# Some elementwise work of a two-layer trunk may go to GpSimd, and a 42-row mask matmul is padded to 128 rows

## The chip, the core and the metric

The program runs on one core of a Trainium2 chip. The metric is the device time of one execution in microseconds. Three executions of the kernel before took 3345.6, 3346.67 and 3353.66 us; the median, 3346.67 us, is what the prediction starts from.

## The reference

Two layers of a latent-diffusion trunk run over 1024 latent tokens and 256 context tokens of width 1024. Each layer normalises and modulates the stream, projects it once with `w_in`, gives the columns to four head groups, joins their outputs with `w_out` and adds them back, and then runs a squared-ReLU MLP of width 4096. Cut to what the change touches:

```python
u = modulate(rms_norm(h, norm1_g), mod[0], mod[1])
pa, pb, pc, pd = jnp.split(u @ w_in, IN_SPLITS, axis=-1)
ya = ssd_bidir(pa)              # Mamba-2 scan by chunks of 128, both directions
yb = attention(rope(norm(q)), rope(norm(k)), v)
a = jnp.exp(log_a)              # RG-LRU
u = jnp.sqrt(-jnp.expm1(2.0 * log_a)) * (i * xr)
h = linear_scan(a, u, h0)
yc = gelu(gate) * (h_fwd + h_bwd)
yd = rms_norm(o1 - lam * o2) * (1 - lam_init)
h = h + mod[2] * (jnp.concatenate([ya, yb, yc, yd], -1) @ w_out)
h = h + mod[5] * (jnp.square(relu(v @ w_mlp1)) @ w_mlp2)
```

The second layer does not update the context tokens.

## The kernel before

**The arithmetic.** Large matmuls are done three times: a float32 operand is split into a high half, rounded to the type fp32r (a one-pass matmul type), and a low half, which is the difference. Then high by high, high by low and low by high are accumulated in one PSUM bank. So each weight block that comes in as `wr` gets a `wh` (a copy with rounding) and a `wl` (a subtraction); this is `split_w` (line 878). Head-group outputs are split in the same way into `yh` and `yl` (`split_mix`, line 1031) or into the two parts of a tile `mo` (`attn_out`, line 1488).

**The stages of a layer.** `ORDER` (line 651) writes them down: the RG-LRU of the first half of its channels, its second half beside the projection of the differential values, the projection `dtq` (step sizes and the queries of the grouped attention), two groups of the SSD, the projections `dk` and `dq`, two rounds of attention, and the output projection in two parts. Then the MLP follows.

- `lru_tile` (line 1092) works on tiles of 128 channels by 1284 columns (latent tokens, a gap, context tokens). For each of two directions it makes gates with ScalarE, then products (`a0 * q`, `thr * a0`, `thi * thr`, in the trace tiles `a` and `th`) and then a scan on VectorE. At the end it forms the gated output `gw`.
- `ssd_group` (line 1190) handles ten chunks in layer 0 and eight in layer 1, for two groups, so 36 chunks. For each chunk a matmul spreads one row of cumulative decays over all partitions. The rows lie in the tile `acr` at partitions 0 to 9 (high halves) and 32 to 41 (low halves); the weights are a one-hot column of `pick`, broadcast. Only 42 partitions take part.
- `qk_post` (line 1297) squares, sums, rotates and transposes queries and keys. The rotation makes two products and adds them (`qkw<-qkw`). The power of -0.5 in every norm runs on GpSimd.

**The order of issue.** Every instruction is first recorded as an operation with an estimated cost in ns. `due` (line 380) gives each a latest time, counted back from TensorE's own order. `run` (line 414) then plays the engines against each other and emits the instructions of each engine in the order found; on the chip every engine's queue is fixed, and semaphores hold the dependences. An operation can have alternatives on two engines (`either`, ScalarE or VectorE). Where an operation is ready, line 512 keeps it back from an engine if another would end it sooner, costs being weighted by `PREF` (line 161):

```python
if any(max(t, free[a], o.ready[a]) + o.alts[a][1] * self.PREF[a]
       < t + o.alts[e][1] * self.PREF[e]
       for a in o.alts if a != e):
```

In the profile all instructions of this planner have one line, L606 (in the order of the changed kernel, L613), since one helper emits them. They are told apart by the names of their tiles; `banks` is PSUM.

Of the kernel before, what the change touches and what calls it, by code (L numbers as in the profile page):

```python
# [11 lines left out]
F32R = mybir.dt.float32r  # L12
AF = mybir.ActivationFunctionType
ALU = mybir.AluOpType
# [141 lines left out]
class Sched:  # L156
# [3 lines left out]
    TABLES = {AF.Sqrt: 1, AF.Exp: 0, AF.Tanh: 0, AF.Abs: 0}  # L160
    PREF = dict(ACT=1.0, DVE=1.6)

# [125 lines left out]

# [1 line left out]
    def act_cost(self, out, in_, func, **kw):  # L290
# [33 lines left out]
    def either(self, out, in_, act, dve):  # L324
        fast = in_.t.cls != "psum"
        a, d = dict(out=out, in_=in_, **act), dve
        ca = self.act_cost(**a)
        cd = self.dve_cost(d[0], fast, **d[1])
        o = self.op("ACT", [("activation", a)], min(ca, cd))
        o.alts = {"ACT": (o.calls, ca), "DVE": ([d], cd)}  # L330
        return o

# [45 lines left out]

# [1 line left out]
    def due(self):  # L380
# [267 lines left out]
class Trunk:  # L648
# [25 lines left out]

# [1 line left out]
    def setup(self):  # L676
        s, A = self.s, self.A
        self.cst = self.const(448, "cst")
        s.dma(self.cst.v, A["cst"])
        c = self.cst  # L680
        self.ident, self.mf, self.mb = c[:, 0:128], c[:, 128:256], c[:, 256:384]
        self.blk2, self.inv_ln, self.inv128 = c[:, 384:386], c[:, 386:387], c[:, 387:388]
        self.nhalf, self.tiny, self.ones32 = c[:, 388:404], c[:, 404:405], c[:, 406:438]
        self.pick = self.const(10, "pick", dt=F32R)[0:42, :]
        s.copy("DVE", self.pick, c[0:42, 438:448])
        self.cT = self.const(8 * 32, "cT")
        self.consts_a(0)
        x = s.tile("h", 512, F32, "load", "cx")
        s.copy("DVE", x[:, 0:16], self.crow)
        s.act(x[:, 16:32], x[:, 0:16], AF.Exp, scale=-1.0)  # L690
        s.ts(x[:, 16:32], x[:, 16:32], 1.0, None, ALU.add)
        s.dve("reciprocal", out=x[:, 16:32], in_=x[:, 16:32])
        s.op("POOL", [("memset", dict(ap=self.cT.v, constant=0.0))], 300)
        s.tt(self.cT.v.r("p (k c) -> p k c", c=32)[:, :, 0:2].r("p k c -> p c k"),
             x[:, 0:16].r("p (c k) -> p c k", c=2), x[:, 16:32].r("p (c k) -> p c k", c=2), ALU.mult)
# [180 lines left out]

# [1 line left out]
    def split_w(self, raw, n):  # L878
        s = self.s
        hi = s.tile("w", WW, F32R, "", "wh")  # L880
        s.copy("ANY", hi[:, 0:n], raw[:, 0:n])
        lo = s.tile("w", WW, F32R, "", "wl")
        s.tt(lo[:, 0:n], raw[:, 0:n], hi[:, 0:n].f, ALU.subtract)
        return hi, lo
# [53 lines left out]

# [1 line left out]
    def load_x(self, gi):  # L940
# [90 lines left out]
    def split_mix(self, k, x, n, stream):  # L1031
        s = self.s
        hi = s.tile("S", SW, F32R, stream, "yh")
        s.copy("ANY", hi[:, 0:n], x[:, 0:n])
        lo = s.tile("S", SW, F32R, stream, "yl")
        s.tt(lo[:, 0:n], x[:, 0:n], hi[:, 0:n].f, ALU.subtract)
        self.save_mix(k, hi, lo, n)
# [9 lines left out]

# [1 line left out]
    def conv(self, out, raw, wcols, bcol, W=CW):  # L1049
# [28 lines left out]

# [1 line left out]
    def lru_weights(self, l):  # L1080
# [11 lines left out]
    def lru_tile(self, l, ct, raw, gate, bd, wy):  # L1092
        s, L = self.s, self.L[l]
        xc = s.tile("S", SW, F32, "lru", "xc")
        self.conv(xc, raw, [L["lcw"][:, 2 * j + ct:2 * j + ct + 1] for j in range(4)], L["lcb"][:, ct:ct + 1])
        hs = []
        W = CW
        for d in range(2):
# [3 lines left out]
            for wi, bn in ((0, "hbr"), (1, "hbi")):  # L1102
                t = s.tile("S", SW, F32, "lru", "th")
                wv = bd[:, 128 * (4 * wi + 2 * d + ct):128 * (4 * wi + 2 * d + ct) + 128]
                for a, b in ((0, 512), (512, 1024), (1024, CW)):
                    pb = s.tile("psum", 512, F32, "lru", "pl")
# [3 lines left out]
            thr, thi = th  # L1110
            m4, p2 = L["m4"][:, idx:idx + 1], L["p2"][:, idx:idx + 1]
            a0 = s.tile("S", SW, F32, "lru", "a0")
# [3 lines left out]
            q = s.tile("S", SW, F32, "lru", "q")  # L1116
            s.stt(q[:, 0:W], thr[:, 0:W], 1.0, a0[:, 0:W], ALU.add, ALU.mult)
            s.affine(q[:, 0:W], q[:, 0:W], -1.0, 2.0)
            s.tt(a0[:, 0:W], a0[:, 0:W], q[:, 0:W], ALU.mult)
            s.act(thr[:, 0:W], thr[:, 0:W], AF.Sqrt, bias=self.tiny)  # L1120
            s.stt(thi[:, 0:W], thi[:, 0:W], 1.0, xc[:, 0:W], ALU.add, ALU.mult)
            s.tt(thr[:, 0:W], thr[:, 0:W], a0[:, 0:W], ALU.mult)
            s.tt(thi[:, 0:W], thi[:, 0:W], thr[:, 0:W], ALU.mult)
            s.affine(a0[:, 0:W], a0[:, 0:W], 2.0, -1.0)
# [19 lines left out]
        g, w = gate[:, 0:wy], s.tile("S", SW, F32, "lru", "gw")  # L1144
        wv = w[:, 0:wy]
        s.act(wv, g, AF.Square)
        s.affine(wv, wv, 0.044715, 1.0)
        s.tt(wv, wv, g, ALU.mult)
        s.act(wv, wv, AF.Tanh, scale=math.sqrt(2.0 / math.pi))
        s.stt(g, wv, 1.0, g, ALU.add, ALU.mult)  # L1150
        s.tt(wv, hs[0][:, 0:wy], hs[1][:, 0:wy], ALU.add)
        s.stt(wv, wv, 0.5, g, ALU.mult, ALU.mult)
        self.split_mix(4 + ct, w, wy, "lru")

# [1 line left out]
    def ssd_dt(self, l, dtraw):  # L1156
        s, L = self.s, self.L[l]
        c = self.ssdc
        dt, dta, w1, w2, w3 = (c[:, 80 * i:80 * i + 80] for i in range(5))
        nac, dec, te = w3, w2, w1  # L1160
        x = dtraw
# [15 lines left out]
        R = s.tile("S", SW, F32R, "ssdr", "acr")  # L1177
        s.op("POOL", [("memset", dict(ap=R[0:42, 0:1024].f, constant=0.0))], 1300)
        n4 = nac.r("p (t d g h) -> p g d h t", t=10, d=2, g=2)
# [10 lines left out]
    def ssd_group(self, l, g, xs, B, C, zmake):  # L1190
# [37 lines left out]
        for i, c in enumerate(order):  # L1228
# [5 lines left out]
            pb = s.tile("psum", 512, F32, "ssd", "pbc")  # L1234
            s.mms([dict(out=pb.v, lhsT=self.pick[:, c:c + 1].bc([42, 128]), rhs=self.acr[0:42, 512 * g:512 * g + 512],
                        start=True, stop=True)])
# [58 lines left out]

# [1 line left out]
    def qk_post(self, l, bank, off, H, d, gain, t, dst, rq=None):  # L1297
# [16 lines left out]
        if t < 8:  # L1314
            j = d // 4
            o = 144 * t + (0 if d == 64 else 96)
            cs = self.rope[:, o:o + d // 2]
            sn = self.rope[:, o + d // 2:o + d + d // 2]
            b4, c4, s4 = (v.r("p (h f k) -> p h f k", h=H, f=2) for v in (b, c, st[:, 0:n]))
            s.tt(c4, b4, cs.un(1).un(1).bc([128, H, 2, 2 * j]), ALU.mult)  # L1320
            s.tt(s4, b4[:, :, ::-1], sn.r("p (f k) -> p f k", f=2).un(1).bc([128, H, 2, 2 * j]), ALU.mult)
            s.tt(b, c, st[:, 0:n], ALU.add)
        y = b
# [49 lines left out]

# [1 line left out]
    def att_open(self, l, kind, idx):  # L1375
# [112 lines left out]
    def attn_out(self, st, b0, nb):  # L1488
# [28 lines left out]
        s.copy("ANY", hi, o[:, 0:n])  # L1517
        s.tt(lo, o[:, 0:n], hi.f, ALU.subtract)
        for d, v in zip(st["mix"], (hi, lo)):
# [9 lines left out]

# [1 line left out]
    def out_proj(self, l, gis, ks):  # L1531
# [242 lines left out]
```

## Time and profile before

| what | value |
|---|---|
| median of three executions | 3346.67 us |
| lowest and highest | 3345.6 and 3353.66 us |
| profiled execution, span from first to last instruction | 3352.2 us |
| TensorE busy | 3258.6 us (97%) |
| VectorE busy | 2171.1 us (65%), 3785 instructions |
| ScalarE busy | 1166.4 us (35%) |
| GpSimd busy | 147.1 us (4%), 168 instructions |
| mean granted TensorE clock | 0.990 |

A profile is of one execution, and the profiled one is a run of its own: its span is 5.5 us above the median of the runs that were timed. Busy time of TensorE is from the start of a matmul to its modelled end, and matmuls overlap, so that the step from one start to the next tells what a matmul really takes. Engines are called PE (TensorE), DVE (VectorE), ACT (ScalarE) and POOL (GpSimd) in the rows.

### The profile page before, as it was taken

What the parts mean: (1) busy time and instruction counts of PE and PEld (TensorE: products, weight loads), DVE (VectorE), ACT (ScalarE), POOL (GpSimd) and SP (SyncE); (2) the same over time, 40 slices, a digit from 0 to 9 for tenths busy, and PEclk for the clock granted to TensorE, in tenths of its full rate; (3) what the DMA queues carried; (4) which work ended last, traced back from release to release, by engine and by line L of the source; (5) the groups of instructions that cost most, each with busy time, mean ns of one, the idle gap of its engine ahead of it and who ended that gap; (6) DMA issues with size and microseconds to landing.
All of it is one profiled execution on the core that took longest, in us unless ns stands there. A gap on an engine that the chain in (4) does not pass through costs nothing. (4 is left out here: it accounts for less than half of the span.)

```text
span 3352.2 us, 45841 instructions
## 1 busy us (share of the span) xinstructions
PE 3258.6 (97%) x18456; PEld 2622.8 (78%) x18456; DVE 2171.1 (65%) x3785; ACT 1166.4 (35%) x2026; POOL 147.1 (4%) x168
## 2 busy tenths in 40 slices
PE   8999989999999999999999999999999999999999
PEld 6877786677688888887887888886677788888887
DVE  4787789894565555554556688689883655555554
ACT  5554447772311110101112554438771311111111
POOL 0010040000000000000000010030000000000000
PEclk9999999999999999999999989989999999999999
DMA  8443261416212222212110321151433111111111
GB/s 247 140 125 97 89 175 41 110 35 232 70 48 75 72 79 67 78 57 85 42 45 26 118 73 50 57 154 39 97 116 121 41 51 51 51 44 46 49 50 57
DMA packets 253868, 276.51 MB, mean 82 GB/s; under 512 B 22876, under 2 KB 212184, under 8 KB 253656
## 3 DMA queue, kind: packets, MB, share of 16 engines
q1 hardware_dynamic: 253656, 273.59, 27.0%
q8 instruction: 145, 2.38, 0.3%
q14 instruction: 67, 0.55, 0.1%
HBM read 218.75 MB, written 54.79 MB: 82 GB/s over the span
## 5 line engine op out<-in xcount | busy, mean ns | idle before, releaser
L606 DVE SCALAR_TENSOR_TENSOR hR<-banks,mod,hR 128x512 f32<-128x512 f32 x720 | 497.2, 697 | 420.4 <-PE banks L606 420.4
L606 PE MATMUL banks<-uh,wh 128*128 128x512 f32 (+1 forms) x1808 | 682.4, 377 | 5.8 <-ACT cvr L606 1.9
L606 PE MATMUL banks<-uh,wl 128*128 128x512 f32 (+1 forms) x1808 | 669.1, 370 | 1.7 <-DVE wl L606 1.7
L606 PE MATMUL banks<-ul,wh 128*128 128x512 f32 (+1 forms) x1808 | 669.0, 370 | 1.3 <-DVE ul L606 1.2
L606 ACT ACTIVATE wh<-wr 128x1024 fp32r<-128x1024 f32 (+2 forms) x193 | 189.5, 992 | 1050.7 <-PE banks L606 1009.9
L606 PE MATMUL banks<-hh,wh 128*128 128x512 f32 (+1 forms) x1280 | 476.7, 372 | 0.0
L606 PE MATMUL banks<-hl,wh 128*128 128x512 f32 (+1 forms) x1280 | 475.5, 371 | 0.0
L606 PE MATMUL banks<-hh,wl 128*128 128x512 f32 (+1 forms) x1280 | 474.8, 371 | 0.0
L606 PEld LDWEIGHTS banks<-uh,wh 128*128 128x128 f32 x1808 | 341.3, 189 | 98.8 <-issue 26.1
L606 PEld LDWEIGHTS banks<-uh,wl 128*128 128x128 f32 x1808 | 340.6, 188 | 65.4 <-DVE wl L606 3.0
L606 PEld LDWEIGHTS banks<-ul,wh 128*128 128x128 f32 x1808 | 341.1, 189 | 61.5 <-DVE ul L606 3.7
L606 DVE TENSOR_SCALAR_CACHE_REDUCE P<-banks,rq 128x1280 f32<-128x1280 f32 (+1 forms) x216 | 301.3, 1427 | 29.4 <-PE banks L606 28.1
L606 DVE TENSOR_TENSOR r<-r 128x512 f32<-128x512 f32 x160 | 102.2, 639 | 333.6 <-ACT r L606 331.4
L606 PEld LDWEIGHTS banks<-hh,wh 128*128 128x128 f32 x1280 | 240.8, 188 | 53.5 <-DVE hR L606 5.3
L606 ACT ACTIVATE P<-P,am 128x1280 f32<-128x1280 f32 (+1 forms) x216 | 273.4, 1272 | 21.1 <-DVE P L606 19.8
L606 PEld LDWEIGHTS banks<-hh,wl 128*128 128x128 f32 x1280 | 240.4, 188 | 44.7
L606 PEld LDWEIGHTS banks<-hl,wh 128*128 128x128 f32 x1280 | 240.6, 188 | 43.3
L606 PE MATMUL banks<-wh,uh 128*128 128x256 f32 (+2 forms) x784 | 250.4, 319 | 6.0 <-DVE qkw L606 4.2
L606 DVE TENSOR_TENSOR wl<-wr,wh 128x1024 fp32r<-128x1024 f32 (+2 forms) x204 | 230.4, 1137 | 27.6 <-ACT wh L606 26.1
L606 PE MATMUL banks<-ks,qt 128*128 128x512 f32 (+1 forms) x800 | 220.8, 387 | 20.2 <-DVE P L606 15.7
L606 PE MATMUL banks<-wl,uh 128*128 128x256 f32 (+2 forms) x784 | 226.3, 289 | 0.0
L606 PE MATMUL banks<-wh,ul 128*128 128x256 f32 (+2 forms) x784 | 225.5, 288 | 0.0
(241 smaller groups left out, 4341.0 us busy)
## 6 DMA issues: line engine op xcount, KB each, us to landing
wr<-in_w_mlp_dram SPq DMA_DIRECT2D x128, 512.0 KB
wm<-in_w_mod_dram SPq DMA_DIRECT2D x96, 512.0 KB
wr<-in_w_in_dram SPq DMA_DIRECT2D x40, 512.0 KB
ks<-dk SPq DMA_DIRECT2D x64, 160.0 KB
qt<-dq SPq DMA_DIRECT2D x72, 128.0 KB
wr<-in_w_out_dram SPq DMA_DIRECT2D x64, 128.0 KB
hd<-hT SPq DMA_DIRECT2D x8, 640.0 KB
ks<-gk SPq DMA_DIRECT2D x16, 320.0 KB
```

The source lines that it names most:

```text
L606: getattr(e, method)(**args)
```

## The change

An operation of two tensors may now be given to VectorE or GpSimd (`tt_any`), where the planner's line 512 takes its choice. The weights of the choice are 1.6 for VectorE and 0.7 for GpSimd, with a cost of 150 + 2.2 n on GpSimd and 69 + 1.0417 n on VectorE for n columns. The low halves in `split_w`, `split_mix` and `attn_out`, five products and sums in `lru_tile` and the sum of the rotation in `qk_post` are recorded in this way. Apart from that, the matmul of the decays takes all 128 rows, with zeros in the added ones.

```diff
-    PREF = dict(ACT=1.0, DVE=1.6)
+    PREF = dict(ACT=1.0, DVE=1.6, POOL=0.7)
+    POOL_TT = 2.2
...
+    def tt_any(self, out, in0, in1, op):
+        o = self.tt(out, in0, in1, op)
+        kw = dict(out=out, in0=in0, in1=in1, op=op)
+        o.alts = {"DVE": (o.calls, o.cost), "POOL": ([("tensor_tensor", kw)], 150 + self.POOL_TT * out.n())}
+        return o
...
-        self.pick = self.const(10, "pick", dt=F32R)[0:42, :]
-        s.copy("DVE", self.pick, c[0:42, 438:448])
+        self.pick = self.const(10, "pick", dt=F32R)
+        s.copy("DVE", self.pick.v, c[:, 438:448])
...
-        s.tt(lo[:, 0:n], raw[:, 0:n], hi[:, 0:n].f, ALU.subtract)
+        s.tt_any(lo[:, 0:n], raw[:, 0:n], hi[:, 0:n].f, ALU.subtract)
...
-            s.tt(a0[:, 0:W], a0[:, 0:W], q[:, 0:W], ALU.mult)
+            s.tt_any(a0[:, 0:W], a0[:, 0:W], q[:, 0:W], ALU.mult)
...
-            s.tt(thr[:, 0:W], thr[:, 0:W], a0[:, 0:W], ALU.mult)
-            s.tt(thi[:, 0:W], thi[:, 0:W], thr[:, 0:W], ALU.mult)
+            s.tt_any(thr[:, 0:W], thr[:, 0:W], a0[:, 0:W], ALU.mult)
+            s.tt_any(thi[:, 0:W], thi[:, 0:W], thr[:, 0:W], ALU.mult)
...
-        s.op("POOL", [("memset", dict(ap=R[0:42, 0:1024].f, constant=0.0))], 1300)
+        s.op("POOL", [("memset", dict(ap=R[:, 0:1024].f, constant=0.0))], 1300)
...
-            s.mms([dict(out=pb.v, lhsT=self.pick[:, c:c + 1].bc([42, 128]), rhs=self.acr[0:42, 512 * g:512 * g + 512],
+            s.mms([dict(out=pb.v, lhsT=self.pick[:, c:c + 1].bc([128, 128]), rhs=self.acr[:, 512 * g:512 * g + 512],
...
-            s.tt(b, c, st[:, 0:n], ALU.add)
+            s.tt_any(b, c, st[:, 0:n], ALU.add)
```

Two more products and sums of `lru_tile` (`wv`) and the low halves in `split_mix` and `attn_out` change in the same words.

What the planner makes of it shows in the engines' queues. On VectorE, in the first direction of the first LRU tile of layer 0, this stood before (`q` and `th` are inputs of the scan, which is the row with two inputs named `a` and `th`):

```order
L606 TENSOR_SCALAR a_433_1040<-a_433_1040 128x1284
L606 SCALAR_TENSOR_TENSOR q_1067<-th_1023,a_433_1040 128x1284
L606 TENSOR_SCALAR q_1067<-q_1067 128x1284
L606 TENSOR_TENSOR a_433_1040<-a_433_1040,q_1067 128x1284
L606 SCALAR_TENSOR_TENSOR th_1038<-th_1038,xc_968 128x1284
L606 TENSOR_TENSOR th_1023<-th_1023,a_433_1040 128x1284
L606 TENSOR_TENSOR th_1038<-th_1038,th_1023 128x1284
L606 COPY vv_1077<-banks 128x256
L606 SCALAR_TENSOR_TENSOR q_1067<-a_433_1040,th_1038 128x256
```

And this stands there now:

```order
L613 TENSOR_SCALAR a_433_1040<-a_433_1040 128x1284
L613 SCALAR_TENSOR_TENSOR q_1067<-th_1023,a_433_1040 128x1284
L613 TENSOR_SCALAR q_1067<-q_1067 128x1284
L613 SCALAR_TENSOR_TENSOR th_1038<-th_1038,xc_968 128x1284
L613 COPY vv_1077<-banks 128x256
L613 TENSOR_SCALAR a_433_1040<-a_433_1040 128x1284
L613 SCALAR_TENSOR_TENSOR th_1129<-th_1129,xc_968 128x1284
L613 SCALAR_TENSOR_TENSOR q_1067<-a_433_1040,th_1038 128x256
```

The three products have left VectorE's queue, and the scan stands behind work of the other direction. They are on GpSimd, between weight halves:

```order
L613 TENSOR_TENSOR wl_1021<-wr_939,wh_1017 128x1024
L613 TENSOR_TENSOR a_433_1040<-a_433_1040,q_1067 128x1284
L613 TENSOR_TENSOR th_1023<-th_1023,a_433_1040 128x1284
L613 TENSOR_TENSOR th_1038<-th_1038,th_1023 128x1284
L613 MEMSET q_1067 128x4
L613 TENSOR_TENSOR a_458_1158<-a_458_1158,q_1193 128x1284
```

In the projection `dq` of layer 0 GpSimd's queue held the powers `rq` alone, one for each tile of tokens. Now the sum of the rotation stands between them:

```order
L613 TENSOR_TENSOR rq_1531<-qkm_4410,cst_66 128x8
L613 TENSOR_TENSOR qkw_4421<-qkw_4421 128x256
L613 TENSOR_TENSOR rq_1531<-qkm_4447,cst_66 128x8
L613 TENSOR_TENSOR qkw_4462<-qkw_4462 128x256
L613 TENSOR_TENSOR rq_1531<-qkm_4492,cst_66 128x8
```

Each sum follows the power of its own tile and stands ahead of the power of the next. Over the whole program 234 operations move from VectorE to GpSimd: 169 low halves of weights (139 of 1024 columns, one of 1056, 29 of 512), 22 products of the LRU (8 `a`, 14 `th`), 3 `gw`, 4 `yl`, 13 `mo` and 23 sums of the rotation. Some copies also change sides: ScalarE's 48 casts `hh` become 3, VectorE's 112 become 157.

## Rows read from the trace of the kernel before

**Rows 1.** The page's first part: busy time and share of the span.
```profile
PE 3258.6 (97%) x18456; PEld 2622.8 (78%) x18456; DVE 2171.1 (65%) x3785; ACT 1166.4 (35%) x2026; POOL 147.1 (4%) x168
```
**Rows 2.** Busy time by stretch: length, engines (instructions), granted clock, DMA share, GB/s.
```profile
84.00:252.00 168.00, 163.63 (x1050) 136.12 (x1049) 133.74 (x195) 90.72 (x131) 17.73 (x26) 0.99 0.41 132
252.00:504.00 252.00, 240.53 (x1640) 201.28 (x1638) 199.16 (x517) 114.24 (x280) 46.20 (x43) 0.96 0.41 121
...
924.00:1764.00 840.00, 840.00 (x4387) 691.66 (x4386) 447.71 (x736) 108.36 (x147) 0.00 (x0) 1.00 0.21 65
1848.00:2016.00 168.00, 162.35 (x941) 137.63 (x941) 123.28 (x182) 89.56 (x133) 15.14 (x17) 0.95 0.30 96
2016.00:2268.00 252.00, 236.90 (x1532) 204.03 (x1530) 204.05 (x505) 111.88 (x264) 41.20 (x42) 0.95 0.31 87
...
2604.00:3276.00 672.00, 669.81 (x2892) 537.20 (x2891) 371.32 (x501) 116.85 (x148) 2.02 (x2) 1.00 0.17 47
```
**Rows 3.** Who TensorE waited for, 84 to 504 us: us, times, longest.
```profile
PE banks L606 <- DVE wk L606: 4.9, 2, 3.8
PE banks L606 <- DVE qkw L606: 3.3, 3, 1.7
```
**Rows 4.** The same view, 1850 to 2268 us.
```profile
PE banks L606 <- DVE qkw L606: 6.7, 6, 2.5
...
PE banks L606 <- DVE wk L606: 2.2, 4, 1.1
```
**Rows 5.** TensorE in order of time, around 2055 us: start, length, matmul.
```profile
2055.07 0.28 PE L606 MATMUL banks<-wl,uh 128*128 128x256 f32 x1
2055.20 0.28 PE L606 MATMUL banks<-wh,ul 128*128 128x256 f32 x1
2055.41 0.49 PE L606 MATMUL banks<-acr,pick 42*128 42x512 f32 x1
2055.82 0.38 PE L606 MATMUL banks<-wh,uh 128*128 128x256 f32 x1
2056.05 0.28 PE L606 MATMUL banks<-wl,uh 128*128 128x256 f32 x1
```
**Rows 6.** The same view, two matmuls of 512 columns on 128 rows.
```profile
2040.75 0.39 PE L606 MATMUL banks<-uh,wh 128*128 128x512 f32 x1
2040.98 0.40 PE L606 MATMUL banks<-ul,wh 128*128 128x512 f32 x1
```
**Rows 7.** Groups by line on TensorE: count | busy us, mean ns | idle before.
```profile
L606 PE MATMUL banks<-uh,wl 128*128 128x512 f32 x1408 | 556.7, 395 | 1.7 <-DVE wl L606 1.7
...
L606 PE MATMUL banks<-acr,pick 42*128 42x512 f32 x36 | 18.0, 501 | 0.7 <-DVE xs L606 0.7
```
**Rows 8.** The same view of VectorE: a weight's low half, an LRU product, the rotation's sum.
```profile
L606 DVE TENSOR_TENSOR wl<-wr,wh 128x1024 fp32r<-128x1024 f32 x168 | 203.4, 1220 | 26.8 <-ACT wh L606 26.1
...
L606 DVE TENSOR_TENSOR qkw<-qkw 128x256 f32<-128x256 f32 x48 | 20.2, 420 | 0.6
...
L606 DVE TENSOR_TENSOR th<-th,th 128x1284 f32<-128x1284 f32 x8 | 11.9, 1494 | 0.2
```
**Rows 9.** The same view of GpSimd: powers of the norms, and a memset.
```profile
L606 POOL TENSOR_TENSOR qkm<-qkm,cst 128x8 f32<-128x8 f32 x20 | 34.0, 1704 | 167.3 <-DVE qkm L606 167.3
...
L606 POOL MEMSET bd<- 128x1024 f32 x2 | 1.9, 952 | 1.0 <-PE banks L606 1.0
```
**Rows 10.** GpSimd in order of time, one power at 161.68 and one at 170.50 us.
```profile
161.68 1.01 POOL L606 TENSOR_TENSOR rq<-qkm,cst 128x4 f32<-128x4 f32 x1 [28.49 <-DVE qkm L606]
...
170.50 2.18 POOL L606 TENSOR_TENSOR rq<-qkm,cst 128x4 f32<-128x4 f32 x1 [3.38 <-DVE qkm L606]
```
**Rows 11.** VectorE in order of time at the second of them.
```profile
170.33 1.49 DVE L606 TENSOR_TENSOR a<-a,q 128x1284 f32<-128x1284 f32 x1
171.73 1.49 DVE L606 SCALAR_TENSOR_TENSOR th<-th,xc 128x1284 f32<-128x1284 f32 x1
```

More of the change, by code (lines that the diff above doesn't have):

```diff
@@ L1035, in split_mix @@
         lo = s.tile("S", SW, F32R, stream, "yl")
-        s.tt(lo[:, 0:n], x[:, 0:n], hi[:, 0:n].f, ALU.subtract)
+        s.tt_any(lo[:, 0:n], x[:, 0:n], hi[:, 0:n].f, ALU.subtract)
         self.save_mix(k, hi, lo, n)
@@ L1147, in lru_tile @@
         s.affine(wv, wv, 0.044715, 1.0)
-        s.tt(wv, wv, g, ALU.mult)
+        s.tt_any(wv, wv, g, ALU.mult)
         s.act(wv, wv, AF.Tanh, scale=math.sqrt(2.0 / math.pi))
         s.stt(g, wv, 1.0, g, ALU.add, ALU.mult)
-        s.tt(wv, hs[0][:, 0:wy], hs[1][:, 0:wy], ALU.add)
+        s.tt_any(wv, hs[0][:, 0:wy], hs[1][:, 0:wy], ALU.add)
         s.stt(wv, wv, 0.5, g, ALU.mult, ALU.mult)
@@ L1517, in attn_out @@
         s.copy("ANY", hi, o[:, 0:n])
-        s.tt(lo, o[:, 0:n], hi.f, ALU.subtract)
+        s.tt_any(lo, o[:, 0:n], hi.f, ALU.subtract)
         for d, v in zip(st["mix"], (hi, lo)):
```

## The prediction, made before the changed kernel had run

> **What bounds the kernel.** I read the page's busy shares first: TensorE is busy 97% of the span, VectorE 65%, GpSimd 4% [rows 1]. So time can go only where TensorE sits idle or runs slowly, and the view by stretch says where that is. In the two MLP stretches TensorE is busy 840.00 of 840 us and 669.81 of 672 us at clock 1.00, while VectorE is at 53 and 55% [rows 2]: work taken off VectorE there buys nothing. What is left are four stretches. In 84:252 and 1848:2016 the RG-LRU runs, VectorE is busy 133.74 and 123.28 of 168 us, and TensorE idles 4.4 and 5.7 us. In 252:504 and 2016:2268 the SSD and the projections `dk` and `dq` run; VectorE has 199.16 and 204.05 of 252 us, and TensorE idles 11.5 and 15.1 us [rows 2]. The view of waits names VectorE's `wk` and `qkw` for 4.9 + 3.3 us in the first half of these and 6.7 + 2.2 us in the second, together 17.1 us [rows 3, 4].
>
> A second loss sits in the same stretches. The clock has two levels, 1.2 and 2.4 GHz; its mean is 0.99, 0.96, 0.95 and 0.95 there [rows 2], and half of full speed is missing whenever it is low: 0.01 x 168 + 0.04 x 252 + 0.05 x 168 + 0.05 x 252 = 32.8 us of lost matmul time. In the MLP, where TensorE never idles, the clock does not fall. So the most that a relief of VectorE could return is 17.1 us of waits and some of the 32.8 us.
>
> **The padding.** Around a 42-row matmul the starts are 2055.20, 2055.41, 2055.82 and 2056.05 [rows 5]: steps of 0.21, 0.41 and 0.23 us. Elsewhere a matmul of 256 columns steps by 0.13 us (2055.07 to 2055.20) [rows 5] and one of 512 columns on 128 rows by 0.23 us [rows 6]. The three steps would be 0.13 + 0.23 + 0.13 = 0.49 instead of 0.85 us, so the odd shape costs 0.36 us, and there are 36 of them [rows 7]: 13.0 us at most. Counting only the matmul's own step (0.41 against 0.23) it is 6.5 us; nothing, if TensorE waits for `wk` behind it anyway. I take 9 us, near the middle of the two counts, since TensorE is busy 95% of 252:504. The memset of `acr` takes all 128 partitions and the same 1024 columns; it costs nothing more, being off every wait.
>
> **The price of a two-input instruction on GpSimd.** The trace has none of more than 10 columns. Its powers take 1704 ns for 8 columns [rows 9], about 0.2 us a column; at that rate a half of 1024 columns would take 200 us. That is the upper end, to which I give no weight: a power is a function to be computed, a subtraction one pass. The memset writes 1024 columns in 952 ns [rows 9], 0.93 ns a column; it reads nothing, so 0.95 us is the lower end. I take three such streams, two read and one written, as the memset is the nearest row: 2.86 us for 1024 columns, 3.58 us for 1284, 0.71 us for 256. VectorE takes 1.22, 1.49 and 0.42 us [rows 8].
>
> The Trainium skill's GPSIMD Engine Reference, section 3.1, gives 4497 ns for an add of 2048 columns, which would be an estimated 2.25 us for 1024 and 2.82 us for 1284 (no run here shows it yet).
>
> **The LRU stretches.** In 84:252, 15 instructions of 1284 columns (11 products, two `gw`, two `yl`) and 7 `wl` leave VectorE: 15 x 1.49 + 7 x 1.22 = 31 us, so it falls from 134 to 103 us. GpSimd gets 15 x 3.58 + 7 x 2.86 = 74 us. In 1848:2016, 11 products, one `gw` and 8 `wl` leave: 27 us, from 123 to 96; GpSimd gets about 65 us. If the two engines ran freely beside each other, that is a clear relief.
>
> Rows speak against that. A power on four columns takes 1.01 us at 161.68, but 2.18 us at 170.50 [rows 10], while VectorE runs a product of two SBUF tiles from 170.33 to 171.82 [rows 11]. The 1.17 us too many are the 1.32 us that this product still had to run, but for a small start-up. VectorE's next instruction, again of two SBUF tiles, ran its usual 1.49 us meanwhile. So GpSimd is held while VectorE reads two tiles. The other direction is not shown, as a power reads only a few columns; I bound it between no hold and a hold for the whole GpSimd instruction. Nearly everything in the LRU reads two SBUF tiles. With some hold, VectorE gives back what it won: saved 31 and 27 us, held for up to 74 and 65. I put the net on the end of the program at 0 in my forecast, and keep both ends, as rivals below.
>
> The Trainium skill (SBUF — State Buffer, section "Who interferes with whom") says that a VectorE instruction with two SBUF inputs and a GpSimd one that reads SBUF exclude each other for a whole instruction, whichever starts first. Rows 10 and 11 agree for the side where VectorE is first; by the full rule the third case below would be the forecast.
>
> **The other moves.** *Rotation sums:* 23 move. In `dq` GpSimd then has 1.70 + 0.71 = 2.4 us a tile, TensorE 24 matmuls of 0.13 us, 3.1 us: it fits, so 0. Behind a late sum stand the next tile's power and, on TensorE, its transposes; if the cover goes, half a microsecond for each of 23 tiles, 12 us. *Weight halves in the MLP:* 110 of 1024 columns. TensorE waited 1.7 us in total for `wl` in the commonest form [rows 7], since halves are made a block ahead, and a block of the first MLP matmul lasts 24 steps of 0.23 us, 5.5 us. An added 1.6 us is covered; without cover it would be 110 x 1.6 = 180 us. GpSimd has nothing else to do there. *`mo`:* 13 halves in attention, read by a store, at nothing. *Casts:* 45 `hh` more on VectorE; at 53 to 55% it has room. No queue of DMA issues is lengthened; the loads of weights wait a little longer for a `wr` tile read by a later half, with a DMA share of 0.17 to 0.21 there [rows 2].
>
> The sum is -9 us. The profiled execution's span of 3352.2 us stands 5.5 us above the median, so I take the difference off the median: 3346.67 - 9 = 3338 us. Its own range is 3326 to 3350.
>
> **Rivals.** *The relief is real* (no hold worth speaking of). VectorE loses a fifth of its load in the LRU; waits and the low clock halve: 8.5 + 16.4 us, with the padding -34 us, 3313 us. For it: VectorE was never slowed by a power. Against: those read next to nothing.
>
> *GpSimd becomes the brake.* The two exclude each other. In 84:252 the remaining 103 us and GpSimd's 74 us make 177, 9 more than the 168 us there are; in 1848:2016, 96 + 65 = 161 fits. Besides, the scans stand behind the products in VectorE's fixed queue: 22 products, each 2.1 us longer, 46 us of which half reaches TensorE, as VectorE also empties PSUM for it. 9 + 23 - 9 = +23 us, 3370 us. It decides from about 3.15 us for a product of 1284 columns, where 103 + GpSimd's share fills the 168 us. For it: rows 10 and 11. Against: the LRU's results are not needed before the output projection, hundreds of microseconds later.
>
> By the skill's 2.82 and 2.25 us GpSimd's share would be 58 us and the 9 us would not arise, which leaves this rival at 3361 us.
>
> *Nothing arrives.* The drains around the 42-row matmuls lie in waits on VectorE, and the moves cancel: 3347 us.
>
> **Chances.** The forecast has 0.45, the relief 0.27, the brake 0.22, nothing 0.06. About 0.3%, 10 us, is what a measurement of this kernel can tell from no change, so 3336.6 and 3356.7 us are the bounds. Of the forecast 0.19 lies below the lower bound and 0.26 between them; the relief gives 0.26 faster, 0.01 same; the brake 0.19 slower, 0.03 same; nothing is 0.06 same. Faster 0.45, same 0.36, slower 0.19. The range takes in both rivals' times with their own slack below: 3306 to 3370 us.
>
> **What would show it.** The decay matmul steps by 0.23 us, and its neighbours by 0.13. GpSimd's products are near 3.6 us, longer where VectorE reads two tiles; VectorE's two-tile instructions of 1.49 us get longer beside them, its PSUM reads do not. TensorE is still busy 840 of 840 us in the MLP. I am wrong if TensorE waits there for `wl`, if VectorE's instructions keep their lengths (the relief), or if waits for `th` or `q` show up in front of VectorE by tens of microseconds (the brake).

## The result, and the profile after

The changed kernel takes 3481.62 us (median of four executions, 3474.56 to 3483.56), the kernel before 3350.16 us on the same chip. The ratio is 1.038 (95% interval 1.0357 to 1.0402): slower by 131 us. The forecast was 3338 us and its range ended at 3370 us, so both its sign and its range are wrong. The profiled execution has a span of 3478.3 us and a mean granted clock of 0.979, against 3352.2 us and 0.990.

The page's first part of the changed kernel answers to [rows 1]:

```profile
PE 3294.4 (95%) x18456; PEld 2647.4 (76%) x18456; DVE 2217.4 (64%) x3612; ACT 1139.6 (33%) x1965; POOL 660.2 (19%) x402
```

GpSimd took 234 operations and 513 us of work. VectorE has 173 instructions fewer, and is busy 46 us *longer*. That is the first surprise. The view by stretch (length, busy time of each engine, granted clock, DMA share, GB/s) answers to [rows 2]; the stages now start later, so the windows of the second layer are shifted with them:

```profile
84.00:252.00 168.00, 144.41 (x909) 119.00 (x908) 129.39 (x184) 78.99 (x115) 78.47 (x47) 0.96 0.43 142
252.00:504.00 252.00, 238.46 (x1609) 201.05 (x1609) 182.94 (x465) 106.15 (x252) 68.13 (x58) 0.95 0.35 103
924.00:1764.00 840.00, 820.36 (x4232) 659.15 (x4231) 454.81 (x686) 117.78 (x163) 135.68 (x57) 0.99 0.21 66
1932.00:2100.00 168.00, 150.48 (x875) 129.83 (x874) 118.19 (x158) 79.65 (x113) 70.98 (x38) 0.93 0.19 56
2730.00:3402.00 672.00, 645.17 (x2699) 518.27 (x2698) 382.30 (x436) 74.62 (x84) 111.25 (x43) 0.97 0.15 44
```

The MLP windows (the third and the fifth) were full at clock 1.00. Now TensorE idles 840 - 820.36 = 19.6 and 672 - 645.17 = 26.8 us there, and the clock is 0.99 and 0.97, which by these two decimals is another 0.01 x 840 + 0.03 x 672 = 28.6 us of matmul time. These two windows alone hold some 75 us; the kernel before lost 2.2 us in them. The LRU windows (first and fourth) idle 23.6 and 17.5 us, where it was 4.4 and 5.7.

The view of waits of TensorE over the whole span (us, times, longest) has a new first row; the kernel before has no row for `hR` at all:

```profile
PE banks L613 <- DVE hR L613: 47.7, 30, 2.0
PE banks L613 <- DVE qkw L613: 28.9, 17, 9.8
```

`hR` is the residual update of the second MLP matmul (in `m2`): VectorE reads a PSUM bank with it, and the bank is free only then. Who makes it late is seen in three timelines around 3026 us, in the MLP of layer 1. GpSimd (start, length, instruction, idle time before and its releaser):

```profile
3025.06 2.70 POOL L613 TENSOR_TENSOR wl<-wr,wh 128x1024 fp32r<-128x1024 f32 x1 [6.25 <-ACT wh L613]
```

VectorE:

```profile
3022.01 0.43 DVE L613 CAST hh<-r 128x512 fp32r<-128x512 f32 x1
...
3024.84 0.69 DVE L613 TENSOR_TENSOR r<-r 128x512 f32<-128x512 f32 x1
3025.56 2.48 DVE L613 CAST hh<-r 128x512 fp32r<-128x512 f32 x1
3027.97 0.74 DVE L613 SCALAR_TENSOR_TENSOR hR<-banks,mod,hR 128x512 f32<-128x512 f32 x1
3028.63 0.68 DVE L613 TENSOR_TENSOR hl<-r,hh 128x512 fp32r<-128x512 f32 x1
```

TensorE:

```profile
3026.23 0.39 PE L613 MATMUL banks<-hl,wh 128*128 128x512 f32 x1
3026.45 0.40 PE L613 MATMUL banks<-hh,wl 128*128 128x512 f32 x1
3028.76 0.78 PE L613 MATMUL banks<-hh,wh 128*128 128x512 f32 x1 [1.91 <-DVE hR L613]
3029.34 0.63 PE L613 MATMUL banks<-hl,wh 128*128 128x512 f32 x1
3029.77 0.63 PE L613 MATMUL banks<-hh,wl 128*128 128x512 f32 x1
...
3032.52 0.40 PE L613 MATMUL banks<-hh,wh 128*128 128x512 f32 x1
3032.76 0.39 PE L613 MATMUL banks<-hl,wh 128*128 128x512 f32 x1
```

The same cast takes 0.43 us at 3022.01 and 2.48 us at 3025.56. It ends at 3028.04, 0.28 us after GpSimd's subtraction (3025.06 + 2.70 = 3027.76). The `hR` that frees the bank stands behind it in VectorE's fixed queue and starts at 3027.97; TensorE has idled for 1.91 us by then. What follows costs nearly as much again: the matmuls step by 0.43 instead of 0.23 us up to about 3032. The view by stretch gives the granted clock for that, 1.2 GHz in the second row and 2.4 GHz in the two beside it:

```profile
3020.00:3026.40 6.40, 6.40 (x29) 5.23 (x28) 4.04 (x6) 1.66 (x2) 1.34 (x1) 1.00 0.23 76
3029.00:3032.00 3.00, 3.00 (x8) 2.32 (x9) 1.25 (x3) 0.00 (x0) 0.00 (x0) 0.50 0.47 164
3033.00:3039.00 6.00, 6.00 (x28) 4.89 (x27) 3.05 (x5) 0.00 (x0) 0.00 (x0) 1.00 0.00 0
```

In this MLP the step of about 2.31 us comes 15 times, every 47 to 48 us. The low clock does not follow every time: it does after 12 of these 15 waits, and in the MLP of layer 0 after two of 14, which last 0.9 to 2.0 us. After the wait that ends at 2885.79, as long as the one shown, the clock stays at its upper level:

```profile
2885.79:2890.29 4.50, 4.50 (x19) 3.68 (x20) 2.72 (x5) 0.00 (x0) 0.00 (x0) 1.00 0.33 117
```

VectorE's groups of 2730 to 3402 us (count | busy us, mean ns | idle before) show what the holds come to:

```profile
L613 DVE SCALAR_TENSOR_TENSOR hR<-banks,mod,hR 128x512 f32<-128x512 f32 x224 | 167.9, 749 | 139.8 <-PE banks L613 139.8
L613 DVE CAST hh<-r 128x512 fp32r<-128x512 f32 x57 | 84.9, 1490 | 1.9
...
L613 DVE TENSOR_TENSOR wl<-wr,wh 128x1024 fp32r<-128x1024 f32 x14 | 36.5, 2608 | 14.8 <-ACT wh L613 14.8
```

In the kernel before, over the whole span, the casts and the `hl` of 256 columns that is met below were these:

```profile
L606 DVE CAST hh<-r 128x512 fp32r<-128x512 f32 x93 | 39.7, 427 | 3.1
...
L606 DVE TENSOR_TENSOR hl<-r,hh 128x256 fp32r<-128x256 f32 x32 | 13.5, 421 | 0.5
```

Casts went from 427 to 1490 ns in the mean and the 14 halves that stayed on VectorE from 1220 [rows 8] to 2608: 57 x 1.06 + 14 x 1.39 = 80 us of hold in a window from which the change took 47 halves of 1.22 us, 57 us. VectorE was not relieved but loaded. `hR`, which reads PSUM, kept its 749 ns.

Which instructions are held, and which are not, is seen side by side at 1418 us. GpSimd:

```profile
1417.76 2.49 POOL L613 TENSOR_TENSOR wl<-wr,wh 128x1024 fp32r<-128x1024 f32 x1 [10.55 <-ACT wh L613]
```

VectorE:

```profile
1417.87 0.74 DVE L613 SCALAR_TENSOR_TENSOR hR<-banks,mod,hR 128x512 f32<-128x512 f32 x1
1418.53 2.00 DVE L613 TENSOR_TENSOR hl<-r,hh 128x256 fp32r<-128x256 f32 x1
```

The first `hR` runs inside GpSimd's subtraction at its usual length. The `hl` behind it, of two SBUF tiles and 256 columns (0.42 us where nothing runs beside it), ends 0.28 us after GpSimd has ended. So the hold is for what remains of the whole GpSimd instruction, and the instruction that reads one operand from PSUM is not held. The Trainium skill (SBUF — State Buffer, "Who interferes with whom") says this of both directions, and counts `cast` and `copy` on VectorE in certain fast modes among the operations that take the shared ports; the trace agrees, with the cast of 2.48 us and the `hl` of 2.00 us above, where GpSimd started first; [rows 10, 11] have the other direction.

Two smaller things of the forecast can be read here. The prices of GpSimd's instructions, which answer to the estimates made from [rows 9]:

```profile
L613 POOL TENSOR_TENSOR wl<-wr,wh 128x1024 fp32r<-128x1024 f32 x139 | 351.1, 2526 | 1644.3 <-ACT wh L613 1616.5 <-PE banks L613 15.7 <-DMA gk<-qkw 7.0
...
L613 POOL TENSOR_TENSOR th<-th,a 128x1284 f32<-128x1284 f32 x8 | 24.2, 3020 | 0.6
```

And the padded matmul, which answers to [rows 5], in TensorE's timeline:

```profile
2246.45 0.28 PE L613 MATMUL banks<-wh,ul 128*128 128x256 f32 x1
2246.57 0.39 PE L613 MATMUL banks<-acr,pick 128*128 128x512 f32 x1
2246.80 0.28 PE L613 MATMUL banks<-wh,uh 128*128 128x256 f32 x1
2246.92 0.28 PE L613 MATMUL banks<-wl,uh 128*128 128x256 f32 x1
```

Its step is 0.23 us and its neighbours' 0.12: 0.47 us for the three, where [rows 5] gave 0.85.

### The profile page after: what moved, and what is told of

Its sections match the earlier page's. It is cut to its first block, busy times and chain, and to the rows that moved or that the text cites. A ratio compares the mean times of both kernels' runs of the same rounds, so it can differ in the third digit from the quotient of the medians.

```text
span 3478.3 us, 45988 instructions
## 1 busy us (share of the span) xinstructions
PE 3294.4 (95%) x18456; PEld 2647.4 (76%) x18456; DVE 2217.4 (64%) x3612; ACT 1139.6 (33%) x1965; POOL 660.2 (19%) x402
## 5 line engine op out<-in xcount | busy, mean ns | idle before, releaser
L613 POOL TENSOR_TENSOR wl<-wr,wh 128x1024 fp32r<-128x1024 f32 (+1 forms) x169 | 391.9, 2319 | 1818.7 <-ACT wh L613 1790.6
L613 PE MATMUL banks<-hh,wh 128*128 128x512 f32 (+1 forms) x1280 | 489.3, 382 | 47.7 <-DVE hR L613 47.7
L613 PE MATMUL banks<-hh,wl 128*128 128x512 f32 (+1 forms) x1280 | 483.8, 378 | 0.0
L613 PE MATMUL banks<-hl,wh 128*128 128x512 f32 (+1 forms) x1280 | 483.5, 378 | 0.0
L613 DVE TENSOR_SCALAR_CACHE_REDUCE P<-banks,rq 128x1280 f32<-128x1280 f32 (+1 forms) x216 | 301.3, 1427 | 26.8 <-PE banks L613 23.4
```

Source lines behind the costliest of these rows:

```text
L613: getattr(e, method)(**args)
```

## The experiments

All kernels below carry the padding. "Above padding alone" is a kernel's difference to the kernel before, measured beside it on the same chip, less that of the padding, -13.6 us. The interval of this -13.6 goes from -18 to -8 us, so that a few us between two kernels say little. The trace alone names a first suspect, the lock in the MLP; rivals are the LRU's late products (the brake of the forecast), the plan (the planner moved casts from ScalarE to VectorE and reordered the queues), and lateness of GpSimd's results.

### Where the time is: five kernels with parts of the change

*Padding alone.* Every `tt_any` of the change is `tt` again, as here in `split_w`:

```diff
-        s.tt_any(lo[:, 0:n], raw[:, 0:n], hi[:, 0:n].f, ALU.subtract)
+        s.tt(lo[:, 0:n], raw[:, 0:n], hi[:, 0:n].f, ALU.subtract)
```

> Padding alone, every two-tensor operation on VectorE. All theories: 5 to 13 us below the kernel before (3337 to 3345 us on its median of 3350), since the decay step fell from 421 to 231 ns 36 times. If it is level, the odd shape's drain lay in a wait anyway.

3338.8 us (3333.49 to 3342.93), ratio 0.996 (0.9945 to 0.9975): -13.6 us, just over the upper of the two counts, 13.0; the lower, 6.5, lies outside the interval. TensorE's busy time falls from 3258.6 to 3245.1 us. No other kernel of the study is clearly faster.

*Only the MLP's weight halves* are free to go; `mlp` is an argument that `m1` and `m2` set.

```diff
-        s.tt_any(lo[:, 0:n], raw[:, 0:n], hi[:, 0:n].f, ALU.subtract)
+        (s.tt_any if mlp else s.tt)(lo[:, 0:n], raw[:, 0:n], hi[:, 0:n].f, ALU.subtract)
```

> Padding, and only the weights' low halves of the two MLPs free to go to GpSimd (108 go). Theory of the lock (a GpSimd subtraction of about 2.5 us holds VectorE's two-tile and copy instructions, and the PSUM evacuations queued behind them come late): the MLP stretches lose 60 to 80 us, so 3400 to 3420 us; TensorE's wait for VectorE's hR of tens of us. Theory of the brake in the LRU: the MLP has room, no more than 15 us above padding alone, so under 3356 us.

3421.14 us, ratio 1.021 (1.0195 to 1.0226): 82 us above padding alone, just over the 60 to 80 us that the lock gave it, and far above the brake's 15. Its view of waits of TensorE begins:

```profile
PE banks L613 <- DVE hR L613: 49.3, 30, 2.1
```

*Everything but the MLP's halves*; the other places stand as in the change.

```diff
-        s.tt_any(lo[:, 0:n], raw[:, 0:n], hi[:, 0:n].f, ALU.subtract)
+        (s.tt if mlp else s.tt_any)(lo[:, 0:n], raw[:, 0:n], hi[:, 0:n].f, ALU.subtract)
```

> Everything as in the change, but the low halves of the MLP weights stay on VectorE (126 two-tensor operations on GpSimd instead of 234). Theory of the lock in the MLP: the MLP is back at 840 busy of 840 us, and what is left is the loss ahead of it, 30 to 50 us above the kernel before: 3380 to 3400 us. Theory of the brake in the LRU: nearly all of the 131 us stays, over 3450 us.

3398.54 us, ratio 1.014 (1.0125 to 1.0155): 60 us above padding alone. The MLP stretches are nearly whole again:

```profile
924.00:1764.00 840.00, 838.63 (x4358) 679.51 (x4357) 459.65 (x752) 123.94 (x177) 2.71 (x3) 1.00 0.22 67
2688.00:3360.00 672.00, 672.00 (x2905) 545.23 (x2904) 363.97 (x488) 100.89 (x124) 0.00 (x0) 1.00 0.16 46
```

The parts add up: -13.6 + 82 + 60 = 128 us, and 131 were measured. The MLP holds the larger share; the brake in the LRU as the sole cause has fallen.

*Only the LRU's products and sums*: `tt_any` stays in `lru_tile` and becomes `tt` in `split_w`, `split_mix`, `qk_post` and `attn_out`; 24 go.

```diff
-            s.tt_any(b, c, st[:, 0:n], ALU.add)
+            s.tt(b, c, st[:, 0:n], ALU.add)
...
-        s.tt_any(lo, o[:, 0:n], hi.f, ALU.subtract)
+        s.tt(lo, o[:, 0:n], hi.f, ALU.subtract)
```

> Padding, and only the LRU's products and sums free to go to GpSimd (24 go, none elsewhere). Lock: each holds a VectorE instruction for up to its own 3 us, 24 x 1.5 to 3 = 36 to 72 us of VectorE time, of which TensorE sees a part: 5 to 30 us above padding alone, 3345 to 3375 us. Brake: 60 us or more above padding alone, over 3400 us.

3372.02 us, ratio 1.0056 (1.0039 to 1.0072): 33 us above padding alone, just over what the lock gave it and far below the brake's 60. The hold is there as well; GpSimd and then VectorE around 182 us:

```profile
181.17 2.94 POOL L613 TENSOR_TENSOR a<-a,q 128x1284 f32<-128x1284 f32 x1 [3.96 <-ACT q L613]
```

```profile
181.28 0.42 DVE L613 TENSOR_TENSOR qkw<-banks,qkw 128x256 fp32r<-128x256 f32 x1
181.62 2.77 DVE L613 TENSOR_TENSOR qkw<-qkw 128x256 f32<-128x256 f32 x1
```

The rotation sum, from two SBUF tiles, takes 2.77 instead of 0.42 us [rows 8]; the one that reads `banks` is not touched. Behind it stand the transposes' inputs, and TensorE's wait for `qkw` is 20.3 us here against 9.4 with padding alone.

*Only the rotation sums, `mo` and `yl`*: `split_w` and the five places of `lru_tile` become `tt`, as in

```diff
-            s.tt_any(a0[:, 0:W], a0[:, 0:W], q[:, 0:W], ALU.mult)
+            s.tt(a0[:, 0:W], a0[:, 0:W], q[:, 0:W], ALU.mult)
```

> Padding, and only the rotation sums (33), the attention's low halves (13) and yl (4) free to go to GpSimd. They are short (0.8 and 1.3 us) and stand beside PSUM work. Lock: 33 x 0.4 + 13 x 0.8 us of hold at most, 24 us of VectorE time, TensorE sees less: 0 to 10 us above padding alone, 3340 to 3355 us. Theory of the late sums: half a microsecond a tile for 33 tiles, 16 us above padding alone or more.

3349.57 us, ratio 0.9992 (0.9983 to 1.0001): 10.5 us above padding alone. Nothing is won; the run lies just over the lock's 10 us and below the 16 us of the late sums, and does not tell them apart. What is left of the 60 us, 60 - 33 - 10.5, some 16 us, is the weight halves outside the MLP or what the parts do to each other (33 sums went here, 23 in the change); it was not tried alone.

### What it is in the MLP: reading, occupying, or the plan

*Memsets in place of subtractions.* GpSimd writes the tile three times, then VectorE forms the half as before.

```diff
+        if mlp:
+            s.op("POOL", [("memset", dict(ap=lo[:, 0:n].f, constant=0.0))] * 3, 2860)
         s.tt(lo[:, 0:n], raw[:, 0:n], hi[:, 0:n].f, ALU.subtract)
```

> Padding alone, plus three memsets on GpSimd over the low-half tile of each MLP weight block (128 blocks, 3 x 0.95 us, writes only), after which VectorE forms the low half as before. GpSimd is as busy at the same places as in the change, and the low half waits for it, but it reads nothing. Theory of the lock by reading two tiles: VectorE's casts, halves and squares keep their 0.43 to 1.2 us, within 10 us of padding alone, about 3340 to 3350 us. Theory of the new plan (the planner moves the casts from ScalarE to VectorE and reorders): the casts move here as well (155 of 160 on VectorE), so most of the 75 us of the MLP shows: 3390 us or more.

3358.68 us, ratio 1.0019 (1.001 to 1.0029): 20 us above padding alone, twice what the lock allowed and far from the 50 and more of the new plan.

*Its twin that reads:*

```diff
-            s.op("POOL", [("memset", dict(ap=lo[:, 0:n].f, constant=0.0))] * 3, 2860)
+            s.op("POOL", [("tensor_tensor", dict(out=lo[:, 0:n], in0=raw[:, 0:n], in1=hi[:, 0:n].f, op=ALU.subtract))], 2530)
```

> The twin of the memset kernel: in the same place GpSimd forms the low half by the subtraction (one pass of about 2.5 us that reads two tiles), and VectorE then forms it once more. Theory of the lock: VectorE's load is that of padding alone, and it is held up to 128 x 2.5 us on top; more than the 75 us of the change's MLP, 3420 to 3480 us. Theory of the new plan: as the memset kernel within 15 us.

3435.92 us, ratio 1.0252 (1.0236 to 1.0267): 97 us above padding alone, 77 above the memset kernel. Both have VectorE's own halves and both have the casts on VectorE (155 and 157 of 160); what differs is that GpSimd reads. Lateness is not it: over the whole span VectorE waits for GpSimd's `wl` less in the twin (second row, 113.1 us) than in the memset kernel (first row, 123.6 us).

```profile
L613 DVE TENSOR_TENSOR wl<-wr,wh 128x1024 fp32r<-128x1024 f32 x168 | 205.1, 1221 | 140.7 <-POOL wl L613 123.6 <-ACT wh L613 16.7
L613 DVE TENSOR_TENSOR wl<-wr,wh 128x1024 fp32r<-128x1024 f32 x168 | 245.0, 1467 | 127.9 <-POOL wl L613 113.1 <-ACT wh L613 14.5
```

With nearly the same instructions (3835 and 3821) VectorE is busy 2218.2 us in the memset kernel and 2357.2 us in the twin, and TensorE waits 3.4 us for `hR` in the one and 56.9 us in the other. For the unexpected 20 us VectorE's groups of the memset kernel, 2646 to 3318 us, show two places:

```profile
L613 DVE TENSOR_TENSOR wl<-wr,wh 128x1024 fp32r<-128x1024 f32 x60 | 73.3, 1221 | 60.0 <-POOL wl L613 60.0
L613 DVE TENSOR_TENSOR hl<-r,hh 128x512 fp32r<-128x512 f32 x61 | 42.0, 688 | 1.5
...
L613 DVE CAST hh<-r 128x512 fp32r<-128x512 f32 x60 | 37.7, 628 | 2.0
```

Beside a GpSimd instruction that only writes, instructions of two tiles keep their 1221 and 688 ns, but the cast goes from 427 to 628 in the mean: 12 us of hold in this window, plus 60 us in which VectorE waits for GpSimd's memsets before its own `wl`. How the 20 us divide between the two was not measured.

*The casts tied to ScalarE*, otherwise the change as it is.

```diff
-                s.copy("ANY", hh[:, g0:g0 + gn], r[:, 0:gn])
+                s.copy("ACT", hh[:, g0:g0 + gn], r[:, 0:gn])
```

> The change, with all 160 casts of the hidden tiles tied to ScalarE (in the change VectorE has 157). Theory that the casts' move is the cause: the MLP loses under 15 us, 3400 us or less. Theory of the lock: the squares and low halves are still held, but fewer instructions stand in the queue: a third to two thirds of the MLP's 78 us comes back, 3430 to 3455 us.

3423.43 us, ratio 1.021 (1.0195 to 1.0225): 61 us faster than the change by the differences to the kernel before, and between the two expectations. The planner also sends 12 of the MLP's 108 halves back to VectorE here; by their number that would be an estimated 9 of the 82 us, not 61. So the casts' place matters more than the lock theory had said. Two more kernels separate them.

*The casts tied to VectorE, nothing added on GpSimd* (against padding alone):

```diff
-                s.copy("ANY", hh[:, g0:g0 + gn], r[:, 0:gn])
+                s.copy("DVE", hh[:, g0:g0 + gn], r[:, 0:gn])
```

> Padding alone, with all 160 casts of the hidden tiles tied to VectorE and nothing added on GpSimd. It asks where the 20 us of the memset kernel come from. If the casts' place by itself costs time: 3350 to 3360 us. If the casts are harmless without GpSimd beside them: within 5 us of padding alone, 3334 to 3344 us, and the 20 us are the copies that the memsets held.

3339.72 us, ratio 0.9963 (0.9951 to 0.9975): level with padding alone. The move of the casts costs nothing by itself.

*The casts tied to ScalarE, only the MLP's halves on GpSimd:* the kernel of 3421 us with the line

```diff
-                s.copy("ANY", hh[:, g0:g0 + gn], r[:, 0:gn])
+                s.copy("ACT", hh[:, g0:g0 + gn], r[:, 0:gn])
```

> Padding, the MLP low halves free to go to GpSimd (96 go), and all 160 casts tied to ScalarE, so that VectorE's queue in the MLP holds only squares, low halves and reads of PSUM. Theory that the casts' place is the cause: level with padding alone, 3334 to 3344 us. Theory of the lock, to which the casts only add instructions that can be held: 15 to 35 us above padding alone, 3354 to 3374 us, with TensorE waiting for hR some 10 to 20 us.

3365.09 us, ratio 1.0035 (1.0024 to 1.0046): 25 us above padding alone, where the kernel with the casts left to the planner, and 108 halves on GpSimd instead of 96, had 82. The hold then falls on the next instruction in the queue; VectorE's groups, 2650 to 3322 us:

```profile
L613 DVE SCALAR_TENSOR_TENSOR hR<-banks,mod,hR 128x512 f32<-128x512 f32 x240 | 178.7, 749 | 131.6 <-PE banks L613 131.6
L613 DVE TENSOR_TENSOR hl<-r,hh 128x512 fp32r<-128x512 f32 x59 | 83.9, 1422 | 30.7 <-ACT hh L613 30.7
...
L613 DVE TENSOR_TENSOR wl<-wr,wh 128x1024 fp32r<-128x1024 f32 x15 | 39.0, 2602 | 16.0 <-ACT wh L613 16.0
```

The hold is still 59 x 0.73 + 15 x 1.38 = 64 us here, not so far below the 80 us of the change. What differs more is the order. Beside a subtraction that runs from 2975.77 for 2.75 us, one `hR` now stands ahead of the held instruction, where in the change the held cast stood ahead of the first:

```profile
2976.21 0.75 DVE L613 SCALAR_TENSOR_TENSOR hR<-banks,mod,hR 128x512 f32<-128x512 f32 x1
2976.94 2.13 DVE L613 TENSOR_TENSOR hl<-r,hh 128x512 fp32r<-128x512 f32 x1
2979.00 1.40 DVE L613 SCALAR_TENSOR_TENSOR hR<-banks,mod,hR 128x512 f32<-128x512 f32 x2
```

TensorE's wait for `hR`, over the whole span, is shorter each time:

```profile
PE banks L613 <- DVE hR L613: 13.7, 19, 0.8
```

The mean clock is 0.991 here, as with padding alone; with 30 waits of up to 2.1 us it was 0.985. So the 82 us have three parts: the lock by GpSimd's reads, a queue in which the held instruction, in layer 1 the cast, stands ahead of the read that frees a PSUM bank, and then the clock. That reading is the cause is shown by the twins; that the order does more than the smaller hold is read from the rows, as no kernel changed the order alone.

### What it is in the LRU, and a false lead

*Unread multiplications.* VectorE makes every product itself; GpSimd multiplies `xc` by itself into a tile that nobody reads, at the places where its products stood. The copy of one column ties the place.

```diff
+            dum = s.tile("S", SW, F32, "lrx", "dum")
+            s.dve("tensor_copy", out=dum[:, 0:1], in_=q[:, 0:1])
+            for _ in range(3):
+                s.op("POOL", [("tensor_tensor", dict(out=dum[:, 0:W], in0=xc[:, 0:W], in1=xc[:, 0:W], op=ALU.mult))], 3000)
```

> Padding alone, VectorE makes every product itself, and GpSimd makes 24 multiplications of 128x1284 in the LRU whose result nobody reads, at the places where its products stood. Nothing can come late from them. Theory of the hold: VectorE loses up to 24 x 3 us and keeps its own products, 25 to 55 us above padding alone, 3364 to 3394 us. Theory of the late products (VectorE waits for GpSimd's results): within 8 us of padding alone, 3331 to 3347 us.

3412.12 us, ratio 1.0178 (1.0156 to 1.0199): 72 us above padding alone. No product can be late here (VectorE's waits for GpSimd are 2.7 us in all, with padding alone 2.8), so lateness is not needed for a loss; but it is more than was expected.

*The write-only twin:*

```diff
-                s.op("POOL", [("tensor_tensor", dict(out=dum[:, 0:W], in0=xc[:, 0:W], in1=xc[:, 0:W], op=ALU.mult))], 3000)
+                s.op("POOL", [("memset", dict(ap=dum[:, 0:W], constant=0.0))] * 3, 3600)
```

> The twin of the kernel with unread multiplications: three memsets of 128x1284 in place of each of the 24, so GpSimd is busy about as long and reads nothing. Theory of the hold by reading: within 10 us of padding alone, 3329 to 3349 us. Theory that GpSimd's short powers behind the long work are the trouble: as its twin within 10 us.

3369.06 us, ratio 1.0049 (1.0031 to 1.0067): 29 us above padding alone, against an expectation of 10 at most. A miss that no theory had foreseen. Two kernels split it. The order without the occupation:

```diff
-                s.op("POOL", [("memset", dict(ap=dum[:, 0:W], constant=0.0))] * 3, 3600)
+                s.op("POOL", [("memset", dict(ap=dum[:, 0:4], constant=0.0))] * 3, 3600)
```

> The write-only twin in the LRU, with the planner told the same 3.6 us for each of the 24 places, so that every engine's order is that of the twin, but each memset writes 4 columns instead of 1284: GpSimd is hardly occupied. Theory that the new order of issue is the cost (the planner keeps powers and what hangs on them back behind work it believes in): the 30 us of the twin stay, 3360 to 3372 us. Theory that the occupied GpSimd makes the powers late: back to padding alone within 8 us, 3331 to 3347 us.

3364.49 us (1.004, 1.0024 to 1.0056): 27 us above padding alone, as the order theory had it. The occupation without the order:

```diff
-                s.op("POOL", [("memset", dict(ap=dum[:, 0:W], constant=0.0))] * 3, 3600)
+                s.op("POOL", [("memset", dict(ap=dum[:, 0:W], constant=0.0))] * 3, 10)
```

> The same twin the other way round: the full memsets of 1284 columns run, but the planner is told 10 ns for each place, so the order is nearly that of padding alone. Order theory: within 8 us of padding alone, 3331 to 3347 us. Theory of the occupied GpSimd: 20 us above it or more, 3359 us or more.

3379.02 us (1.0081, 1.0064 to 1.0097): 42 us above, as the theory of the occupied GpSimd had it. Order alone and occupation alone both cost, which fits neither theory by itself; what both share is the wide tile `dum`. So a control with the tile and neither:

```diff
-                s.op("POOL", [("memset", dict(ap=dum[:, 0:W], constant=0.0))] * 3, 3600)
+                s.op("POOL", [("memset", dict(ap=dum[:, 0:4], constant=0.0))] * 3, 10)
```

> A control for the four twins: the same extra tile and the same small copy on VectorE, but 4-column memsets and 10 ns told to the planner, so neither occupation nor belief. If it is within 5 us of padding alone (3334 to 3342 us), the twins' 27 to 42 us belong to the order and to the occupied queue. If it is 20 us or more above (3359 us or more), the extra tile, which takes one of the 30 wide tiles from the rest, is what costs, and the twins' times are to be taken against this control.

3358.26 us (1.0017, 1.0008 to 1.0027): 19 us above padding alone, a hair under the 20 us of its expectation, with nothing added on GpSimd but 4-column memsets. And the order without the tile:

```diff
-            dum = s.tile("S", SW, F32, "lrx", "dum")
+            dum = self.dum
...
-                s.op("POOL", [("memset", dict(ap=dum[:, 0:W], constant=0.0))] * 3, 3600)
+                s.op("POOL", [("memset", dict(ap=dum[:, 0:4], constant=0.0))] * 3, 3600)
```

> The planner is told 3.6 us for each of 24 places on GpSimd, the memsets write 4 columns, and no wide tile is taken (the 4 columns lie in a small constant tile). Order theory: 15 to 30 us above padding alone, 3354 to 3369 us. If the wide tile was the cost: within 8 us, 3331 to 3347 us.

3339.84 us (0.9964, 0.9951 to 0.9977): level with padding alone. So the order theory falls, and some 19 us of each twin go with the wide tile that it takes from the rest. Taken against the control with the tile, as if the tile cost the same in each, the unread multiplications cost 53 us, the write-only memsets 10, the order alone 8, and the memsets that the planner does not know of 23. In that last kernel VectorE waits 11.8 us for GpSimd's memsets themselves, so it does not show that powers come late. Between the twins, GpSimd's reads cost 43 us for 24 instructions of 75.4 us in all, though the memsets keep GpSimd busy for longer, 87.7 us. The pages' first parts, of the kernel that reads and then of the one that writes, have the same 42 us in VectorE's busy time:

```profile
PE 3267.5 (96%) x18456; PEld 2637.5 (77%) x18456; DVE 2219.3 (65%) x3796; ACT 1166.7 (34%) x2023; POOL 226.2 (7%) x192
PE 3253.5 (97%) x18456; PEld 2627.2 (78%) x18456; DVE 2177.3 (65%) x3797; ACT 1167.0 (35%) x2022; POOL 238.3 (7%) x240
```

The kernel with the real products loses 33 us though VectorE is spared 24 x 1.49 = 36 us of work; VectorE is even busy 10.9 us longer, 2180.3 us against 2169.4 with padding alone. The hold gives back what the move saved, and the waits for results come on top. In its view of waits VectorE stands 10.0 us for `th` and 3.2 us for `gw` from GpSimd. How the 33 us divide between hold and these waits stays open. So does why one of 30 wide tiles is worth 19 us.

## Why the prediction was wrong

**The padding** was right: -9 us forecast, -13.6 measured, and the count of all three steps (13.0) was the better one of the two.

**The price of a GpSimd instruction** was somewhat high: 2.86 us for 1024 columns against 2.53 in the mean, 3.58 for 1284 against 3.0 to 3.5. Nothing of the outcome hung on it.

**"Weight halves in the MLP at nothing: an added 1.6 us is covered"** is the step that failed, and with it "TensorE is still busy 840 of 840 us in the MLP". Its lateness was costed rightly: TensorE waits 2.4 us in all for a `wl` from GpSimd. But only the lateness was. The hold between the engines, read from [rows 10, 11] and weighed for the LRU, was not carried over to the MLP, although VectorE's queue there holds casts, squares and halves from SBUF with reads of PSUM between them. Nor did the prediction have a hold for a cast, which reads one tile; in the MLP of layer 1 the held instruction was mostly one. "GpSimd has nothing else to do there" was true and beside the point: what counts is what VectorE does meanwhile. Put at nothing, the 108 halves (the prediction counted 110) measured 82 us alone.

**"Casts: 45 `hh` more on VectorE; it has room"** was right by itself (the kernel with the casts on VectorE is level) and wrong together with the halves: of the 82 us, 57 go when the casts are on ScalarE, with 96 halves on GpSimd instead of 108.

**"I put the net on the end of the program at 0"** for the LRU is the second step that failed. The direction left open turned out to be a whole hold, as the section of the Trainium skill named above has it. The net on VectorE's busy time was indeed small, the 10.9 us above. But the holds hit `qkw`, for which TensorE waits 10.9 us longer, TensorE's mean clock fell from 0.991 to 0.987, and the time rose by 33 us. The rival of the brake gave 3370 us, and the kernel with the LRU's part alone takes 3372. That is luck: the rival's sum was for the whole change, and counted weight halves that this kernel does not move. Its mechanism is half right: the view of waits shows 13 us for late results, and the trace shows holds of rotation sums that it had not named.

**Rotation sums and `mo` at 0** were 10.5 us together with `yl`, inside the 12 us named as their upper end.

**The clock** was expected to hold in the MLP, since TensorE never idled there; once it idled, for up to 2 us at a time, the 1.2 GHz level followed 14 of the 29 waits for `hR` of 0.9 us or more.

The relief (3313 us) found nothing to relieve: VectorE's instructions beside GpSimd did not keep their lengths.

## What to carry to other kernels

Work handed to GpSimd is not free because GpSimd is idle: in these runs, while it read SBUF, VectorE's casts and its instructions with two SBUF inputs stood still until it ended, and everything behind them in VectorE's queue with them. Before moving an elementwise operation there, list what VectorE does beside it, and look for the instruction that frees a PSUM bank behind a held one. A planner that gives each engine its own cost needs a price for the two together; here its choice by single costs made the kernel 131 us slower, and 145 us slower than the padding alone, 3338.8 us, which beats both kernels.

## What the hardware showed that was not expected

- A VectorE cast of 512 columns is held for the rest of a GpSimd subtraction (0.43 to 2.48 us), and also, for less, beside a GpSimd memset (427 to 628 ns in the mean), which leaves instructions of two SBUF tiles alone (688 and 1221 ns).
- A wait of TensorE of 1.91 us in the middle of a full MLP is followed by 3 us at a granted clock of 0.50, at the step of 0.43 us that goes with it; the stop then costs nearly twice its length. This followed 12 of the 15 such waits of one MLP and not the other three, which are as long; what decides it stays open.
- Taking one of 30 wide tiles from the planner for the time of an LRU direction cost 19 us with no work added to speak of; the cause was not followed.
